# A trunk of convolution and gated recurrence on one core: 32 bytes of padding behind the input tiles and the split weight tiles

## The chip, the cores and the metric

The kernel runs on one core of a Trainium2 chip. The metric is the device time of one execution in microseconds (us). The matrix engine is called PE or TensorE (its weight loads are listed apart, as PEld), the vector engine DVE, the scalar engine ACT, the general engine POOL, and SP issues the DMAs.

## The reference

The reference computes one decoder layer on 1024 tokens of width 1024 in float32. Cut to what matters here:

```python
u = rms_norm(h, ln_g[i])
z = u @ w_in[i]                       # 1024 x 1024 by 1024 x 7168
c_val, c_glu, c_gate, hq, hf, hi, hg = jnp.split(z, split_pts, axis=-1)
y_conv = conformer_conv_branch(c_val, c_glu, c_gate, ...)   # 31 taps, then y @ w_pw2
y_hgrn = hgrn2_branch(hq, hf, hi, hg, ...)                  # 8 heads of 128
h = h + jnp.concatenate([y_conv, y_hgrn], axis=-1) @ w_out[i]
pe = p[i] @ w_pp[i]
gate = jax.nn.sigmoid(rms_norm(h, pe_norm_g[i]) @ w_pg[i])
return rms_norm(h + gate * pe, final_g)
```

Five of these lines hold large matrix products: with `w_in`, `w_pw2`, `w_out`, `w_pp` and `w_pg`.

## The kernel before

**Products in three parts.** A float32 operand of a large product is split into two float32r tiles, a high part `hi` (a rounded copy, made on ACT at L113) and a low part `lo` (the rest, made on DVE at L114). A product is the sum of three matmuls, high by high, high by low and low by high. Every one of these matmuls loads a 128 x 128 block of weights (the stationary operand) and streams 512 columns of float32r past it (the moving operand); for the values of the heads it is 256 columns.

**Where the operands lie.** The input of the layer, normalised and transposed, is held in 32 tiles `uh` and `ul` of 128 partitions by 512 numbers, so of 2048 bytes a partition. They are made in `norm_x` (L173, L174) and come from the pool `up`, which has 32 places under the tag "u". A weight block is made by `prep` (L116 to L123): a `raw` tile, into which SP loads 4096 bytes a partition, and a tile `hi` and a tile `lo` of the same size. Each of these three tags has 3 places in the pool `wp`. Places of one tag lie one behind the other, so they step by 2048 bytes in `up` and by 4096 bytes in `wp`. The slices that the matmuls take out of these tiles begin at multiples of 512 bytes. So do the slices of the tiles of the later stages, which come from `up` and from a third pool, `yp` (L545 to L552, tiles of 2048 bytes).

**Stages.** (1) The layer embedding `p` is multiplied by `w_pp` (L228 to L230) and x is normalised and transposed. (2) In the z stage, head by head, `ztile` takes 128 columns of `w_in` and `product` (L235) multiplies them into two banks of 512 tokens each: 16 rounds of the three matmuls at L241, L242 and L243, with `wh` or `wl` as weights and `uh` or `ul` moving. The values (`values`, L263 to L265) have the roles the other way round: `uh` or `ul` are the weights, and 256 columns of the weight tiles move. Between these products stand the small float32 matmuls of the recurrence (`hgrn`: L295, L383, L409, L426, L427) and transposes (L399, L441, L462, L482). DVE computes the convolution with 29 instructions a head at L452, of which each reads its source `vpad` 4 bytes further on than the one before, and ACT does the activations. (3) `product` again, with `w_pw2` (tiles `pw`). (4) `w_out`, in `accumulate` (L588, L589, L591). (5) `w_pg` (L682 to L684), the gate and the last normalisation.

**What sets the order.** A scheduler orders the instructions of each engine when the program is built. A weight block's load and split are put ahead of time with a raised priority. All large loads are issued by SP's queue. The program reserves 16,384 bytes a partition of the on-chip memory as a scratch area for DMA descriptors; this is the default of the builder called at L715.

Of the kernel before, what the change touches and what calls it, by code (L numbers as in the profile page):

```python
# [16 lines left out]
P = 128  # L17
T = 1024          # tokens
D = 1024          # model width
G = 8             # channel groups, heads, 128-row blocks of T and D  # L20
TAPS = 31
PAD = TAPS - 1
H = 512           # half a row of 1024: one PSUM bank of float32
EPS = 1e-6
# Order of the work of each head and channel group: projections of the GLU gate (u), conv value
# (c), forget gate (f), query (q), values of two heads (v), output gate (g); conv (C); HGRN (H).
ORDER = ("ucfgqvCH", "ucfgqCH") * (G // 2)
# How much later than traced the scheduler takes work that waits on a chain of small steps.
LATER_STATS, LATER_CONV, LATER_HEAD = 50, 330, 240
# columns of the transposed parameter table  # L30
R_CB, R_CG, R_CBETA, R_BPW, R_L0, R_L1, R_ON, R_LN, R_PE = range(TAPS, TAPS + 9)
# [4 lines left out]
def trunk_kernel(ctx: ExitStack, tc: tile.TileContext, x, p, ln_g, w_in, conv_w, conv_b,  # L36
# [25 lines left out]

    # ---------------------------------------------------------------- constants
    ident = cst.tile([P, P], F32, name="ident")
# [5 lines left out]

    # per-channel parameters, channels on partitions
    par = cst.tile([P, G, NR], F32, name="par")
# [3 lines left out]
    def load_params(work):  # L76
        rows = work.tile([NR, D], F32, name="prow")
        nc.sync.dma_start(rows[0:TAPS, :], conv_w[0])
        for r, ap in ((R_CB, conv_b), (R_CG, cnorm_g), (R_CBETA, cnorm_b), (R_BPW, b_pw2),
                      (R_ON, onorm_g), (R_LN, ln_g), (R_PE, pe_norm_g)):  # L80
            nc.sync.dma_start(rows[r:r + 1, :], ap)
        nc.sync.dma_start(rows[R_L0:R_L0 + 2, :], lb_logits)
        pt = bank("t", "pt")
        for g in range(G):
            nc.tensor.transpose(pt[:, g * NR:(g + 1) * NR], rows[:, g * P:(g + 1) * P],
                                ident[:NR, :NR])
        nc.vector.tensor_copy(par, pt[:, :G * NR].rearrange("p (g r) -> p g r", r=NR))
        # lower bound: first row of the softmax over the layers
        l0, l1 = par[:, :, R_L0], par[:, :, R_L1]
        mx = cst.tile([P, G], F32, name="lmx")  # L90
        e0 = cst.tile([P, G], F32, name="le0")
        e1 = cst.tile([P, G], F32, name="le1")
        nc.vector.tensor_tensor(mx, l0, l1, op=ALU.max)
        nc.vector.tensor_tensor(e0, l0, mx, op=ALU.subtract)
        nc.vector.tensor_tensor(e1, l1, mx, op=ALU.subtract)
        nc.scalar.activation(e0, e0, AF.Exp)
        nc.scalar.activation(e1, e1, AF.Exp)
        nc.vector.tensor_tensor(e1, e0, e1, op=ALU.add)
        nc.vector.reciprocal(e1, e1)
        nc.vector.tensor_tensor(lbt, e0, e1, op=ALU.mult)  # L100
        nc.vector.tensor_scalar(oml, lbt, -1.0, 1.0, op0=ALU.mult, op1=ALU.add)
# [14 lines left out]
    def prep(src, shape, name):  # L116
        """A weight block: loaded, and split exactly into two float32r parts."""
        raw = wp.tile(shape, F32, tag="raw", name=name)
        nc.sync.dma_start(raw, src)
        hi = wp.tile(shape, F32R, tag="hi", name=name + "h")  # L120
        lo = wp.tile(shape, F32R, tag="lo", name=name + "l")
        split(hi, lo, raw)
        return hi, lo  # L123
# [6 lines left out]

    # ---------------------------------------------------------------- z phase
    uh = [[None] * G, [None] * G]
    ul = [[None] * G, [None] * G]
    with tc.tile_pool(name="st", bufs=1) as st:
        # layer embedding, projected: kept in DRAM until the gate is known
        KP = p.shape[1] // P
# [29 lines left out]
        def norm_x(hf, xs):  # L166
            """Normalised input of four token blocks, channels on partitions, split."""
            for k in range(G):
                pt = bank("t", f"ut{hf}_{k}")
                for b in range(4):  # L170
                    nc.tensor.transpose(pt[:, b * P:(b + 1) * P], xs[b][:, k * P:(k + 1) * P],
                                        ident)
                uh[hf][k] = up.tile([P, H], F32R, tag="u", name=f"uh{hf}_{k}")  # L173
                ul[hf][k] = up.tile([P, H], F32R, tag="u", name=f"ul{hf}_{k}")  # L174
                nc.scalar.activation(uh[hf][k], pt, AF.Copy, scale=pcol(k, R_LN))
# [5 lines left out]
        load_params(st)  # L181
        # masks[l][s, col]: where the key s is one that the score column couples to, the columns
        # being those of the block of 32 that s lies in
        ones = st.tile([P, 4 * 48], F32, name="ones")
        nc.gpsimd.memset(ones, 1.0)

        def block_mask(dst, first, step_n, step_j, l):
            """Sets dst[s, n, j, i] where s is in the l keys from first + n step_n + j step_j."""
            src = ones[:, :dst.shape[1] * dst.shape[2] * l].rearrange(
# [9 lines left out]
        def own_block(name, mf):  # L199
            """The columns of each row's own block out of those of the four blocks of 32."""  # L200
            n = mf.shape[1] // 4
            own = st.tile([P, n], F32, name=f"own{name}")
            nc.vector.tensor_reduce(own, mf.rearrange("p (b n) -> p n b", b=4), op=ALU.add,
                                    axis=mybir.AxisListType.X)
            msk = cst.tile([P, n], U8, name=f"mask{name}")
            nc.vector.tensor_copy(msk, own)
            return msk
# [27 lines left out]
    def product(wh, wl, mh, ml, tag, name):  # L235
        """Two banks [128 columns of w, 512 tokens] of w^T m."""
        res = []
# [14 lines left out]
    def values(idx, vt):  # L252
        """Two column tiles of z with tokens on partitions."""
        with tc.high_priority(2000):
# [25 lines left out]
    def hgrn(h, QD, K, F, vt, sgT):  # L280
        A, B = AT[h % 2], AB
        # Decayed scores. A level couples the later blocks of l tokens in a parent block to the
        # earlier ones: queries carry the decay since their block of l began (and over the
        # blocks in between), keys the decay until their block of l ends, so that every factor
        # is at most one.
        # Levels within blocks of 32: every block's scores take 48 columns, on its own 32
        # partitions, and go to B[s, chunk, t mod 32].
        blocks = T // 32

        def scores(l, rhs):  # L290
            pt = bank("t", f"sc{h}_{l}")
            pv = pt[:, :G * 48].rearrange("p (c w) -> p c w", c=G)
            for b in range(blocks):
# [4 lines left out]

        # Diagonal and pairs: the keys are the same.
        q01 = QD[:, :, :32].rearrange("p b (n j two) -> p b n j two", j=4, two=2)  # L300
# [9 lines left out]
                                  pv[:, :, 32:])  # L310
        # queries of a level of four blocks: per parent, its blocks 0..3, then 2 and 3 decayed
        # over one more block, then 3 over two more
        Q = wk.tile([P, 7 * T // 4], F32, tag="Q", bufs=2, name=f"Q{h}_2")
# [4 lines left out]
        def pair_keys(l, Fl):  # L318
            """Widens the keys' blocks from l to 2l; the decay over each block of 2l."""
            n = T // (2 * l)  # L320
# [9 lines left out]
        for l in (2, 8):  # L330
# [14 lines left out]
            for d0, j0, cnt in ((1, 0, 3), (2, 3, 2), (3, 5, 1)):  # L345
# [4 lines left out]
                    pv[:, :, :, js])  # L350
            # widen to blocks of 4l
            Q4 = wk.tile([P, 7 * T // 4], F32, tag="Q", bufs=2, name=f"Q{h}_{4 * l}")
# [24 lines left out]
        for l in (32, 64):  # L377
# [14 lines left out]
            Fl = pair_keys(l, Fl)  # L392
        # state after each chunk
        kt = wk.tile([P, G, P], F32, tag="kt", name=f"kt{h}")
# [145 lines left out]

    # ---------------------------------------------------------------- pointwise projection
    yp = ctx.enter_context(tc.tile_pool(name="yp", bufs=32, reuse_waits="tile"))
# [33 lines left out]

    # ---------------------------------------------------------------- output projection
    hs = [hp.tile([P, D], F32, name=f"h{tb}") for tb in range(G)]
# [3 lines left out]
    def accumulate(zs, hf, k, wh, wl, first, last):  # L582
        """zs: {(token block, column half): bank}."""
        for b in range(4):
# [34 lines left out]
    def norm_T(hf):  # L619
        """Scaled residual of 4 token blocks, channels on partitions, split; its RMS in rs."""  # L620
        hh = [None] * G
# [34 lines left out]

    # ---------------------------------------------------------------- gated layer embedding
    gh = [[None] * G, [None] * G]
# [8 lines left out]
    for tb in range(G):  # L667
# [5 lines left out]
        ot = wp.tile([P, D], F32, tag="lo", name=f"ot{tb}")  # L673
        # the last block ends in narrower pieces, so that less work follows the last product
        pieces = (H, H) if tb < G - 1 else (H, H // 2, H // 2)
# [54 lines left out]
```

## Time and profile before

| | us |
|---|---|
| median of the 2 runs | 1147.24 |
| the 2 runs | 1146.36 and 1148.12 |
| span of the profiled execution | 1146.5 |

The page of the profiled execution gives its span from the first to the last instruction; the two timed runs lie within 1.6 us above it and 0.2 us below it, so no time of note lies around the span. In a row of a profile, "L241" is line 241 of the kernel, "xN" a count, "out<-in" the tiles written and read (of a matmul: output, then moving operand and weights). A matmul's listed duration includes the time in which its last columns run through the array, and the next one starts before it ends: what a stream of matmuls costs is read from start to start.

### The profile page before, as it was taken

What the parts mean: (1) busy time and instruction counts of PE and PEld (TensorE: products, weight loads), DVE (VectorE), ACT (ScalarE), POOL (GpSimd) and SP (SyncE); (2) the same over time, 40 slices, a digit from 0 to 9 for tenths busy, and PEclk for the clock granted to TensorE, in tenths of its full rate; (3) what the DMA queues carried; (4) which work ended last, traced back from release to release, by engine and by line L of the source; (5) the groups of instructions that cost most, each with busy time, mean ns of one, the idle gap of its engine ahead of it and who ended that gap; (6) DMA issues with size and microseconds to landing.
All of it is one profiled execution on the core that took longest, in us unless ns stands there. A gap on an engine that the chain in (4) does not pass through costs nothing.

```text
span 1146.5 us, 17744 instructions
## 1 busy us (share of the span) xinstructions
PE 1124.8 (98%) x7408; PEld 945.6 (82%) x7408; DVE 739.5 (65%) x1145; ACT 443.0 (39%) x811; POOL 72.0 (6%) x107
## 2 busy tenths in 40 slices
PE   6999999999999999999999999999999999999997
PEld 4888978889888789788898788888888888887886
DVE  3659579998499996599993896242334325226444
ACT  4823244253354442344532632442123324126333
POOL 3100001001001010010010010000000001001000
PEclk9899999999999999999999999999999999999999
DMA  7611121211111112111111112277335632334221
GB/s 247 236 37 55 37 66 30 74 55 39 55 57 56 59 35 74 56 37 56 57 56 56 57 56 93 74 242 254 110 92 165 195 99 77 107 109 149 92 92 56
DMA packets 85715, 104.60 MB, mean 91 GB/s; under 512 B 3290, under 2 KB 65754, under 8 KB 85634
## 3 DMA queue, kind: packets, MB, share of 16 engines
q1 hardware_dynamic: 85634, 103.46, 28.1%
q8 instruction: 58, 0.95, 0.3%
q14 instruction: 23, 0.19, 0.1%
HBM read 82.48 MB, written 20.97 MB: 90 GB/s over the span
## 4 chain that ended last, share of the span: by engine, by line
PE 89%; DVE 6%; DMA 2%; ACT 1%; issue 1%; SPq 0%; POOL 0%; POOLq 0%; ACTq 0%
PE z L241 14%; PE z L242 14%; PE z L243 14%; DVE y L452 4%; PE v L264 3%; PE v L265 3%; PE v L263 3%; PE pg L683 3%; PE pg L684 3%; PE pg L682 3%; PE oA L591 3%; PE pw L243 3%; PE pw L241 3%; PE oA L589 3%; PE oA L588 3%; PE pw L242 3%
## 5 line engine op out<-in xcount | busy, mean ns | idle before, releaser
L452 DVE SCALAR_TENSOR_TENSOR y<-vpad,par,y 128x1024 f32<-128x1024 f32 x232 | 288.8, 1278 | 1.1
L682 PE MATMUL pg<-gh,hh 128*128 128x512 f32 (+1 forms) x136 | 51.4, 378 | 0.0
L683 PE MATMUL pg<-gl,hh 128*128 128x512 f32 (+1 forms) x136 | 51.4, 378 | 0.0
L684 PE MATMUL pg<-gh,hl 128*128 128x512 f32 (+1 forms) x136 | 51.3, 377 | 0.0
L519 DVE TENSOR_TENSOR vpad<-z,gl 128x512 f32<-128x512 f32 x16 | 11.0, 691 | 42.7 <-PE z L243 42.7
L263 PE MATMUL v<-wv_0h,uh 128*128 128x256 f32 x128 | 36.7, 287 | 0.0
L265 PE MATMUL v<-wv_0h,ul 128*128 128x256 f32 x128 | 36.5, 285 | 0.0
L264 PE MATMUL v<-wv_0l,uh 128*128 128x256 f32 x128 | 36.5, 285 | 0.0
L263 PE MATMUL v<-wv_1h,uh 128*128 128x256 f32 x128 | 36.2, 283 | 0.0
L264 PE MATMUL v<-wv_1l,uh 128*128 128x256 f32 x128 | 36.2, 283 | 0.0
L265 PE MATMUL v<-wv_1h,ul 128*128 128x256 f32 x128 | 36.2, 283 | 0.0
L266 ACT ACTIVATE vt<-v 128x256 f32<-128x256 f32 x32 | 12.2, 382 | 58.9 <-PE v L265 58.9
L688 DVE TENSOR_TENSOR gt<-gt,pet 128x512 f32<-128x512 f32 (+1 forms) x17 | 11.2, 661 | 36.1 <-ACT gt L687 36.1
L108 POOL TENSOR_SCALAR ro<-sso 128x8 f32<-128x8 f32 x8 | 8.4, 1054 | 389.9 <-ACT on L129 389.9
L475 DVE TENSOR_SCALAR y<-yt,mv,ry 128x128 f32<-128x128 f32 x64 | 23.5, 404 | 13.1 <-POOL ry L109 13.1
L570 DVE SCALAR_TENSOR_TENSOR sgr<-pw,par,sgr 128x512 f32<-128x512 f32 x16 | 12.0, 750 | 30.1 <-PE pw L243 30.1
L437 ACT ACTIVATE on<-o,ro 128x128 f32<-128x128 f32 x64 | 18.5, 386 | 29.0 <-POOL ro L109 29.0
L682 PEld LDWEIGHTS pg<-gh,hh 128*128 128x128 f32 x136 | 25.6, 188 | 4.7
L683 PEld LDWEIGHTS pg<-gl,hh 128*128 128x128 f32 x136 | 25.6, 188 | 4.7
L684 PEld LDWEIGHTS pg<-gh,hl 128*128 128x128 f32 x136 | 25.6, 188 | 4.5
L483 ACT ACTIVATE yc<-yn,par 128x512 f32<-128x512 f32 x16 | 12.5, 778 | 39.8 <-PE yn L482 39.8
L129 ACT ACTIVATE on<-o 128x128 f32<-128x128 f32 x64 | 16.9, 278 | 23.3 <-PE up L409 18.9
(802 smaller groups left out, 3463.6 us busy)
## 6 DMA issues: line engine op xcount, KB each, us to landing
wz<-in_w_in_dram SPq DMA_DIRECT2D x48, 512.0 KB
wo<-in_w_out_dram SPq DMA_DIRECT2D x32, 512.0 KB
xt<-in_x_dram SPq DMA_DIRECT2D x8, 512.0 KB
pe_d<-pes SPq DMA_DIRECT2D x8, 512.0 KB
wv<-in_w_in_dram SPq DMA_DIRECT2D x8, 512.0 KB
yc_d<-yc SPq DMA_DIRECT2D x8, 512.0 KB
yh_d<-sgT SPq DMA_DIRECT2D x8, 512.0 KB
sg_d<-sgc SPq DMA_DIRECT2D x8, 512.0 KB
```

The lines of the kernel that those rows point to most:

```text
L241: mm(z, lhsT=wh[:, k, :], rhs=mh[hf][k], start=k == 0, stop=False)
L242: mm(z, lhsT=wh[:, k, :], rhs=ml[hf][k], start=False, stop=False)
L243: mm(z, lhsT=wl[:, k, :], rhs=mh[hf][k], start=False, stop=k == G - 1)
L263: mm(z, lhsT=uh[hf][k][:, c], rhs=wh, start=k == 0, stop=False)
L264: mm(z, lhsT=uh[hf][k][:, c], rhs=wl, start=False, stop=False)
L265: mm(z, lhsT=ul[hf][k][:, c], rhs=wh, start=False, stop=k == G - 1)
L452: nc.vector.scalar_tensor_tensor(y[j % 2], vp[:, j:j + T], pcol(g, j), y[j % 2], op0=ALU.mult, op1=ALU.add)
L588: mm(z, lhsT=mixh[hf][k][:, c], rhs=wh[j], start=first, stop=False)
L589: mm(z, lhsT=mixh[hf][k][:, c], rhs=wl[j], start=False, stop=False)
L682: mm(z, lhsT=hh[k][:, c], rhs=gh[j][k][:, o:o + w], start=k == 0, stop=False)
L683: mm(z, lhsT=hh[k][:, c], rhs=gl_[j][k][:, o:o + w], start=False, stop=False)
L684: mm(z, lhsT=hl[k][:, c], rhs=gh[j][k][:, o:o + w], start=False, stop=k == G - 1)
```

## The change

The tiles `uh` and `ul` get 8 float32 more than they use, so their 32 places step by 2080 bytes. The tiles `hi` and `lo` of `prep` are made as flat tiles of 1032 numbers and cut back to 1024, so their 3 places step by 4128 bytes. Views of the same shape as before are taken of them, and every instruction works on the same elements. The `raw` tiles and the tiles of `yp` keep their size. The descriptor scratch goes from 16,384 to 2,048 bytes a partition, which makes room: the program took all but some 600 of the bytes of a partition before, and the padding needs 38 times 32 = 1216. Every tile behind the scratch area moves down accordingly. Later tiles that use the places of "u", "hi" and "lo" (`mc`, `hh`, `hl`, `gt`, `ot`) start where those places start. In the built program before, the moving operand and the weights of each of the 4,728 float32r matmuls begin at addresses that differ by a multiple of 512 bytes; after the change that holds for 206 of them, 2,232 differ by an even multiple of 32 bytes (206 among them) and 2,496 by an odd one. The operands of the float32 matmuls and transposes (L399, L409) lie in other pools and differ by no multiple of 512 before. The instructions of each engine and their order stay as they were (6272 matmuls of the program in the same order, as all others), and so do the semaphores that they wait for.

```diff
+STEP = 8
...
     def prep(src, shape, name):
         raw = wp.tile(shape, F32, tag="raw", name=name)
         nc.sync.dma_start(raw, src)
-        hi = wp.tile(shape, F32R, tag="hi", name=name + "h")
-        lo = wp.tile(shape, F32R, tag="lo", name=name + "l")
+        n = shape[1] if len(shape) == 2 else shape[1] * shape[2]
+        hi = wp.tile([P, n + STEP], F32R, tag="hi", name=name + "h")[:, :n]
+        lo = wp.tile([P, n + STEP], F32R, tag="lo", name=name + "l")[:, :n]
+        if len(shape) == 3:
+            hi, lo = (t.rearrange("p (k c) -> p k c", k=shape[1]) for t in (hi, lo))
         split(hi, lo, raw)
         return hi, lo
...
-                uh[hf][k] = up.tile([P, H], F32R, tag="u", name=f"uh{hf}_{k}")
-                ul[hf][k] = up.tile([P, H], F32R, tag="u", name=f"ul{hf}_{k}")
+                uh[hf][k] = up.tile([P, H + STEP], F32R, tag="u", name=f"uh{hf}_{k}")[:, :H]
+                ul[hf][k] = up.tile([P, H + STEP], F32R, tag="u", name=f"ul{hf}_{k}")[:, :H]
...
-    nc = _bacc.Bacc("TRN2", target_bir_lowering=False, num_devices=1)
+    nc = _bacc.Bacc("TRN2", target_bir_lowering=False, num_devices=1,
+                    dynamic_dma_scratch_size=2048)
```

## Rows read from the trace of the kernel before

**Rows 1.** The page: span, and busy time, share and instructions of each engine.

```profile
span 1146.5 us, 17744 instructions
...
PE 1124.8 (98%) x7408; PEld 945.6 (82%) x7408; DVE 739.5 (65%) x1145; ACT 443.0 (39%) x811; POOL 72.0 (6%) x107
```

**Rows 2.** The page: shares of the chain that ended last, by engine.

```profile
PE 89%; DVE 6%; DMA 2%; ACT 1%; issue 1%; SPq 0%; POOL 0%; POOLq 0%; ACTq 0%
```

**Rows 3.** Busy time by stretch: length, engines (instructions), granted clock, DMA share, GB/s.

```profile
0.00:30.00 30.00, 19.26 (x77) 15.06 (x78) 11.83 (x23) 13.44 (x21) 11.38 (x30) 0.96 0.79 251
...
315.00:415.00 100.00, 99.62 (x933) 81.71 (x933) 96.22 (x149) 47.25 (x85) 5.70 (x4) 1.00 0.17 54
...
760.00:860.00 100.00, 100.00 (x443) 82.84 (x442) 36.20 (x46) 26.68 (x38) 0.00 (x0) 1.00 0.52 171
```

**Rows 4.** Timeline in the z stage: start us, us, engine, line, operation, tiles.

```profile
142.04 0.39 PE L243 MATMUL z<-uh,wz1l 128*128 128x512 f32 x1
142.04 0.19 PEld L241 LDWEIGHTS z<-uh,wz1h 128*128 128x128 f32 x1
142.27 0.39 PE L241 MATMUL z<-uh,wz1h 128*128 128x512 f32 x1
...
149.97 0.39 PE L242 MATMUL z<-ul,wz1h 128*128 128x512 f32 x1
```

**Rows 5.** Timeline of the values' matmuls, 256 columns wide.

```profile
105.77 0.28 PE L263 MATMUL v<-wv_0h,uh 128*128 128x256 f32 x1
105.77 0.19 PEld L264 LDWEIGHTS v<-wv_0l,uh 128*128 128x128 f32 x1
...
106.73 0.28 PE L265 MATMUL v<-wv_0h,ul 128*128 128x256 f32 x1
```

**Rows 6.** Eight transposes in the timeline, and the line's own view (min/median/max ns).

```profile
175.33 1.03 PE L399 MATMUL ktp<-ident,K 128*128 128x128 f32 x8
...
L399 PE MATMUL ktp<-ident,K x64: 270/272/273, 175.3 to 723.5; 128*128 128x128 f32 x64
```

**Rows 7.** Whole span, one line each of L228, L241, L263, L588, L682 (count behind PE).

```profile
0.00:1146.50 1146.50, 14.07 (x32) 6.63 (x32) 1.00 0.29 91
0.00:1146.50 1146.50, 356.76 (x896) 168.41 (x896) 1.00 0.29 91
0.00:1146.50 1146.50, 72.93 (x256) 49.11 (x256) 1.00 0.29 91
0.00:1146.50 1146.50, 99.88 (x256) 48.08 (x256) 1.00 0.29 91
0.00:1146.50 1146.50, 51.41 (x136) 25.60 (x136) 1.00 0.29 91
```

**Rows 8.** Weight loads by line and shape: busy us, mean ns, idle before.

```profile
L241 PEld LDWEIGHTS z<-uh,wz26h 128*128 128x128 f32 x16 | 3.0, 189 | 0.6
...
L409 PEld LDWEIGHTS up<-vt,kt 128*128 128x128 f32 x112 | 20.6, 189 | 4.2 <-ACT kt L401 0.3
```

**Rows 9.** DVE: the convolution's line (min/median/max ns) and one split, by line.

```profile
L452 DVE SCALAR_TENSOR_TENSOR y<-vpad,par,y x232: 1264/1278/1290, 75.1 to 685.1; 128x1024 f32<-128x1024 f32 x116
...
L114 DVE TENSOR_TENSOR wz48l<-wz,wz48h 128x1024 fp32r<-128x1024 f32 x1 | 1.2, 1226 | 7.3 <-ACT wz48h L113 7.3
```

**Rows 10.** DMA queues: packets, MB, share of 16 engines.

```profile
q1 hardware_dynamic: 85634, 103.46, 28.1%
```

## The prediction

> **What bounds the kernel now.** I read the page's busy times first, then the chain that ended last, then busy time by stretch, and then single matmuls in the timeline. The reader is to see that PE is busy for 1124.8 of 1146.5 us [rows 1] and holds 89% of the chain; DMA has 2% of it [rows 2]. By stretch it is the same: PE is busy for 99.62 of 100 us in the middle of the z stage and for all of 100 us in the `w_out` stage [rows 3]. DVE comes near only in places (96.22 of the 100 us from 315), and the DMA engines only in the opening, at a share of 0.79 [rows 3]. So the change can win or lose only by what it does to the distance between matmuls, or by making another engine so much slower that it overtakes PE.
>
> That distance is the number of the case. In the z stage the matmuls at 142.04 and 149.97 us are the ends of 35 steps (L241 to L243 in turn) [rows 4]: 7.93 / 35 = 226.6 ns a step. At the granted clock of 1.00, that is 2.4 GHz, 512 columns stream in 213.3 ns, so 13.3 ns of each step is something else. The values stream 256 columns (106.7 ns), and 8 steps take 106.73 - 105.77 = 0.96 us [rows 5], 120 ns each: again 13.3 ns over. Eight transposes of 128 columns, which are float32 and pass twice (106.7 ns), end after 1.03 us of which the last one's own duration is 0.272 [rows 6]: (1030 - 272) / 7 = 108.3 ns a step, only 1.6 ns over. So float32r matmuls pay about 11.7 ns more than these do.
>
> **The change part by part.** It removes and adds no instruction, no transfer and no wait, and it moves none. What it can change is how long an instruction takes at its new addresses, and how DMAs are issued with a smaller scratch. The sum is made against the profiled execution, 1146.5 us, which is 0.7 us below the median of the runs, 1147.24; I put its difference on the median.
>
> *Matmuls.* There are 3 x (32 + 896 + 256 + 256 + 136) = 4,728 of float32r, since each row stands for one of a stage's three lines [rows 7]. Before, the two operands of every one of them lie a multiple of 512 bytes apart, and the weights of the next matmul begin to load at the same 0.01 us at which the current one starts to stream (142.04 and 142.04, 105.77 and 105.77) [rows 4, 5]. If the two streams, starting in step, collide in the memory, the 11.7 ns could be that collision, and the change would end it. If it belongs to float32r itself, the change does nothing. The trace of before can't settle this, because no float32r matmul in it has operands out of step, and the transposes differ in both respects. So I bound it from both sides by the nearest rows: gain at most 4,728 x 11.7 = 55.3 us; loss at most as much again as today's overhead for those matmuls whose operands lie an odd multiple of 32 apart, 2,496 x 13.3 = 33.2 us.
>
> I take zero, for three reasons. The overhead is the same 13.3 ns for a stream of 2048 bytes as for one of 1024 bytes, so it goes with the instruction and not with how long the two streams run beside each other. The 35 steps also run through weight slices that lie 512, 1024 and 1536 bytes apart within 2048, and still come to one mean that equals the values'. And a weight load takes 189 ns in the z stage, in step, and 189 ns at L409, where the operands lie out of step [rows 8]; if two reads held each other up I would expect the load to show some of it.
>
> On this place the Trainium skill has two rules that pull apart. "TensorE: Matmul & The Clock Gate", section "Back-to-back issue gap", gives a step of N / 2.4 + 2.5 ns at full clock, which is 215.8 ns for 512 columns; by it 226.6 is too long and the sum would be an estimated 4,728 x 10.8 = 51 us of avoidable time, which bears out the collision. The same page, section "Step-by-step: what each phase is for", says that loading the next weights takes no read bandwidth from the running matmul because PE has two read ports; by it there is no collision and the sum is zero. The trace agrees with the first for the transposes (1.6 ns over) and contradicts it for float32r, which the page's figure was not measured on.
>
> *DVE and ACT.* The 166 splits on DVE now read or write a tile that may begin 32 bytes off a multiple of 64. DVE shows no sign of caring: at L452 the source moves by 4 bytes from one instruction to the next, through 29 different places, and all 232 durations lie between 1264 and 1290 ns [rows 9]. A spread of 2% on a split of 1226 ns would be 25 ns, times 166 is 4 us of DVE in 1146, where DVE is busy 65% [rows 1]; PE's work covers it. I put it at zero; where the cover is thin, from 315 to 415 us, DVE has 3.8 us left [rows 3], and a seventh of 4 us fits. For ACT, which only writes the padded tiles, I see no row that would say otherwise, and it is busy 39%.
>
> *The scratch.* All 85,634 packets of the kernel's transfers go through one queue that the page calls hardware_dynamic [rows 10]. Whether it keeps anything in the scratch area the trace doesn't show. If not, the cost is zero, which I take, because DMA is 2% of the chain and its share is under a fifth for most of the z stage [rows 2, 3].
>
> The sum is 0 + 0 + 0: 1147 us, and its own range, from the runs' spread and the few us of the covered terms, is 1143 to 1152.
>
> **The rivals.**
>
> *A: the collision is real, and any shift of phase ends it.* Then all but 206 of 4,728 matmuls lose 11.7 ns: 52.9 us, so 1094. For it speaks that 13.3 ns goes with in-step operands wherever it is seen and 1.6 ns with out-of-step ones, and that PE has nothing else in its way. Against it, the three reasons above. In the z stage DVE would take some of it back: from 315 us on PE would need about 95 of 100 us where DVE needs 96.2 [rows 3], which costs 1 or 2 us. I say 1095.
>
> *B: the collision is real, but depends on the position within 64 bytes only.* Then the 2,496 matmuls at an odd multiple of 32 are freed: 2,496 x 11.7 = 29.2 us, so 1118. The same rows speak for it, and the finer the pattern in memory, the less the equal overhead of all slices says against it.
>
> *C: starts off a multiple of 64 bytes cost a restart.* Here the 2,496 matmuls with one operand 32 bytes off pay the overhead twice: 33.2 us, so 1180, slower. The place is every stage, the price is 13.3 ns, and it decides from 22.9 / 2,496 = 9 ns a matmul, where the time passes 2%. Against it: nothing of the kind shows on DVE at any of 29 places [rows 9]; PE's float32r stream may still have less slack than DVE's.
>
> *D: the smaller scratch throttles the DMAs*, so that the change does something else than it says. The opening is the place: its first 30 us run at a DMA share of 0.79, and PE is busy for only 19.26 of them [rows 3]. At half the rate 24 us of transfers become 48, so up to 24 us more there; the `w_out` stage at 0.52 [rows 3] would just be covered. That is 1171, and it needs a queue held to half its rate.
>
> **How the numbers follow.** A difference of under 2%, 23 us, is about what a measurement of this kernel can tell from no change. My forecast, no change, has 0.69; A 0.11 and B 0.13; C 0.04 and D 0.03. A and B both end over 2% faster (1095 and 1118 against 1124.3), so faster is 0.24. C and D at their full price end over 2% slower (1180 and 1171 against 1170.2): 0.07. The same is 0.69. The range goes down to 1116, which takes in B, and leaves A out; upward to 1158, about a third of C's price, which leaves out 0.05 or so. What is left out is 0.16 to 0.18. The predicted time is that of the likeliest case, 1147.
>
> **What would show it right or wrong.** If I am right, the timeline of the z stage still has a step of 226 to 227 ns for every pair of tiles, whichever places they have, the weight loads still take 188 or 189 ns, and the splits 1226. If A or B is right, steps near 215 ns appear: under A for nearly all, under B for every other place, so that lines with `uh` and with `ul` moving differ. If C is right, steps near 240 ns appear for the same half. If D is right, matmuls are untouched and the DMA share of the opening falls while PE's idle time there grows. Any change in the step of float32r matmuls by more than 5 ns over most tiles makes the prediction wrong.

## The result, and the profile after

The changed kernel takes 1159.12 us (median of 2 runs, 1159.01 to 1159.23) against 1147.24 us before: 11.9 us more, a ratio of 1.0106 with a 95% interval of 1.0089 to 1.0122. That is less than 2%, but its interval leaves 1 out, and the time lies 1 us above the range that was forecast. No difference was forecast.

Of the page after, the span, the busy times, the chain by engine and the DMA queue stand here beside [rows 1], [rows 2] and [rows 10]; the lines of the program are 4 further on than before.

```profile
span 1157.5 us, 17744 instructions
...
PE 1140.0 (98%) x7408; PEld 945.3 (82%) x7408; DVE 738.7 (64%) x1145; ACT 443.1 (38%) x811; POOL 72.6 (6%) x107
...
q1 hardware_dynamic: 85634, 103.46, 27.8%
...
PE 89%; DVE 6%; DMA 2%; ACT 1%; issue 0%; SPq 0%; POOLq 0%; POOL 0%; ACTq 0%
```

Instructions, packets and megabytes are the same. The span is 11.0 us longer and PE is busy for 15.2 us more, while weight loads, DVE, ACT and POOL moved by less than 1 us, and the shares of PE, DVE and DMA in the chain did not move. So the time went into PE's matmuls and nowhere else. The same three stretches as in [rows 3]:

```profile
0.00:30.00 30.00, 21.10 (x78) 16.34 (x79) 12.10 (x23) 13.74 (x24) 11.40 (x30) 0.96 0.77 251
...
315.00:415.00 100.00, 99.77 (x929) 81.15 (x928) 95.83 (x149) 46.64 (x85) 5.70 (x4) 1.00 0.17 54
...
760.00:860.00 100.00, 100.00 (x433) 80.88 (x432) 37.01 (x49) 27.55 (x41) 0.00 (x0) 1.00 0.54 177
```

The reader is to look at the counts and not at the busy shares: in the `w_out` stage PE is busy for all of 100 us in both kernels, but gets through 433 matmuls where it got through 443. That is 230.9 ns each for 225.7. The granted clock is 1.00 in both, so the engine isn't slower, its matmuls stand further apart. The opening moves as many GB/s as before (251) at the same DMA share within 0.02.

In the z stage, the timeline has these two matmuls, with 25 others between them and no gap; they answer to [rows 4]:

```profile
144.86 0.39 PE L245 MATMUL z<-uh,wz1h 128*128 128x512 f32 x1
...
150.88 0.39 PE L247 MATMUL z<-uh,wz1l 128*128 128x512 f32 x1
```

26 steps in 6.02 us are 231.5 ns a step, where before they were 226.6. Over the whole span, the first lines of the four products (L245, L267, L592, L686) answer to [rows 7]:

```profile
0.00:1157.50 1157.50, 360.45 (x896) 168.52 (x896) 1.00 0.28 90
...
0.00:1157.50 1157.50, 72.33 (x256) 48.24 (x256) 1.00 0.28 90
...
0.00:1157.50 1157.50, 101.17 (x256) 48.09 (x256) 1.00 0.28 90
...
0.00:1157.50 1157.50, 51.82 (x136) 25.55 (x136) 1.00 0.28 90
```

Three of them grew and the values shrank. Summed over the three lines of each triple, z and `w_pw2` together took 9.1 us more, `w_out` 3.6, `w_pg` 1.5, and the values 1.7 less: 12.5 us, which covers the 11.9 that were measured. (The lines of `w_pp` are busy for 2.0 us more, in the opening; from start to start they take 0.4 us less.) The weight loads, the convolution and the split of [rows 8] and [rows 9]:

```profile
L245 PEld LDWEIGHTS z<-uh,wz26h 128*128 128x128 f32 x16 | 3.0, 189 | 0.6
...
L456 DVE SCALAR_TENSOR_TENSOR y<-vpad,par,y 128x1024 f32<-128x1024 f32 x232 | 288.8, 1278 | 1.1
...
L115 DVE TENSOR_TENSOR wz48l<-wz,wz48h 128x1024 fp32r<-128x1024 f32 x1 | 1.2, 1226 | 7.5 <-ACT wz48h L114 7.5
```

All as before: 189 ns, 1278 ns, 1226 ns. The listed duration of a matmul does move: 395 ns here, 389 ns for the same 16 matmuls before. First after, then before:

```profile
L245 PE MATMUL z<-uh,wz3h 128*128 128x512 f32 x16 | 6.3, 395 | 0.0
...
L245 PE MATMUL pw<-ych,wpw3h 128*128 128x512 f32 x16 | 6.3, 393 | 0.0
```

```profile
L241 PE MATMUL z<-uh,wz3h 128*128 128x512 f32 x16 | 6.2, 389 | 0.0
```

Where nothing interrupts the stream, the step is this duration less about 162 ns (389 - 226.6 before), so the column of mean durations shows the step of every tile at a glance. It is used below.

### The profile page after: what moved, and what is told of

It is laid out like the page before. It is cut to its first block, busy times and chain, and to the rows that moved or that the text cites. A ratio compares the mean times of both kernels' runs of the same rounds, so it can differ in the third digit from the quotient of the medians.

```text
span 1157.5 us, 17744 instructions
## 1 busy us (share of the span) xinstructions
PE 1140.0 (98%) x7408; PEld 945.3 (82%) x7408; DVE 738.7 (64%) x1145; ACT 443.1 (38%) x811; POOL 72.6 (6%) x107
## 4 chain that ended last, share of the span: by engine, by line
PE 89%; DVE 6%; DMA 2%; ACT 1%; issue 0%; SPq 0%; POOLq 0%; POOL 0%; ACTq 0%
PE z L245 14%; PE z L246 14%; PE z L247 14%; DVE y L456 4%; PE v L267 3%; PE v L268 3%; PE v L269 3%; PE pw L245 3%; PE pg L688 3%; PE pw L246 3%; PE pg L687 3%; PE oA L592 3%; PE oA L595 3%; PE pg L686 3%; PE oA L593 3%; PE pw L247 3%
## 5 line engine op out<-in xcount | busy, mean ns | idle before, releaser
L456 DVE SCALAR_TENSOR_TENSOR y<-vpad,par,y 128x1024 f32<-128x1024 f32 x232 | 288.8, 1278 | 1.1
L686 PE MATMUL pg<-gh,hh 128*128 128x512 f32 (+1 forms) x136 | 51.8, 381 | 0.0
L267 PE MATMUL v<-wv_0h,uh 128*128 128x256 f32 x128 | 36.4, 284 | 0.0
L267 PE MATMUL v<-wv_1h,uh 128*128 128x256 f32 x128 | 35.9, 281 | 0.0
L270 ACT ACTIVATE vt<-v 128x256 f32<-128x256 f32 x32 | 12.2, 383 | 57.7 <-PE v L269 57.7
L686 PEld LDWEIGHTS pg<-gh,hh 128*128 128x128 f32 x136 | 25.6, 188 | 5.2
L487 ACT ACTIVATE yc<-yn,par 128x512 f32<-128x512 f32 x16 | 12.5, 779 | 40.5 <-PE yn L486 40.5
```

Source lines behind the costliest of these rows:

```text
L267: mm(z, lhsT=uh[hf][k][:, c], rhs=wh, start=k == 0, stop=False)
L456: nc.vector.scalar_tensor_tensor(y[j % 2], vp[:, j:j + T], pcol(g, j), y[j % 2], op0=ALU.mult, op1=ALU.add)
L686: mm(z, lhsT=hh[k][:, c], rhs=gh[j][k][:, o:o + w], start=k == 0, stop=False)
```

## The experiments

**1. Matmuls alone, with the distance of the operands as the only variable (map1).** Groups of 20 float32r matmuls into one bank, with the same two operands each time, the weights taken `s` and the moving operand `m` numbers into two tiles that begin a multiple of 256 bytes apart. Groups differ in `s` (wshift, 32 bytes a group; fine, 4 bytes), in `m` (mshift), in both (both), in the columns (narrow: 256), or take two slices in turn (turns, turnm). A matmul is called in step here when its weights and its moving operand begin a multiple of 256 bytes apart.

```python
for r in range(rep):
    m, s = mv[r % len(mv)], st[r % len(st)]
    mm(z[:, :n], lhsT=W[:, s:s + P], rhs=X[:, m:m + n], start=r == 0, stop=r == rep - 1)
...
    z = group(f"wshift{chr(97 + i // 16)}{chr(97 + i % 16)}", [0], [8 * i])
...
    z = group(f"mshift{chr(97 + i)}", [8 * i], [0])
...
    z = group(f"both{chr(97 + i)}", [8 * i], [8 * i])
...
    z = group(f"narrow{chr(97 + i)}", [0], [8 * i], n=256)
```

> A kernel of float32r matmuls alone (the trunk is left out, its output is one bank's numbers): groups of 20 matmuls of 512 columns, each with its own weight load; from group to group the weight slice, the moving slice or both begin 32 bytes (in one series 4 bytes) further on. Theory 1, the two reads of PE meet in the memory, so the step depends on how far apart they begin: 'both' groups all alike at the 226.6 ns of the kernel before, 'wshift' and 'mshift' groups between 224 and 238 ns, the same values at the same distance. Theory 2, starts that are not multiples of 64 bytes cost by themselves: every second group slower by some 5 to 10 ns, in 'both' as in the others. Theory 3, neither, the padding isn't the cause: 226.6 ns in all groups of 512 columns.

In the timeline, a group is one row: its start, and its busy time from the first start to the last end, which is 19 steps and one duration. The weights begin 0, 32, 256 and 288 bytes behind the moving operand:

```profile
26.94 4.70 PE L57 MATMUL wshiftaa<-X,W 128*128 128x512 f32 x20
...
31.48 4.82 PE L57 MATMUL wshiftab<-X,W 128*128 128x512 f32 x20
...
64.07 4.70 PE L57 MATMUL wshiftai<-X,W 128*128 128x512 f32 x20
...
68.61 4.82 PE L57 MATMUL wshiftaj<-X,W 128*128 128x512 f32 x20
```

(4.70 - 0.389) / 19 = 226.9 ns and (4.82 - 0.395) / 19 = 232.9 ns: 32 bytes cost 6 ns, and 256 bytes bring the old step back. From the starts of the single matmuls, the mean steps by the distance of the weights behind the moving operand, modulo 256 bytes, are (an entry moves by up to 0.7 ns with the choice of which steps of a group are averaged):

| bytes | 0 | 32 | 64 | 96 | 128 | 160 | 192 | 224 |
|---|---|---|---|---|---|---|---|---|
| 512 columns, ns | 226.7 | 233.3 | 233.3 | 234.7 | 232.2 | 233.6 | 228.7 | 233.3 |
| 256 columns, ns | 120.0 | 118.4 | 117.8 | 117.2 | 118.9 | 119.9 | 113.3 | 116.6 |

The pattern repeats every 256 bytes up to 1024. Moving the other operand gives the mirror image within about 1 ns (228.8 where it stands 64 bytes on). Moving both alike leaves 226 to 227 ns, after some seven steps of 223 to 236 ns at a group's start; so it is not the starts by themselves that count (theory 2), and theory 3 is out as well. In steps of 4 bytes, up to 60, only the distance 0 gives 226.7, all others 230 to 235. With two slices in turn, those 256 bytes apart settle at 226.7. The rows by line and shape show the width's part: at 0 and at 192 bytes the narrow groups have

```profile
L57 PE MATMUL narrowa<-X,W 128*128 128x256 f32 x20 | 2.6, 283 | 0.0
...
L57 PE MATMUL narrowg<-X,W 128*128 128x256 f32 x20 | 2.4, 276 | 0.0
...
L57 PEld LDWEIGHTS wshiftab<-X,W 128*128 128x128 f32 x20 | 3.8, 188 | 0.9
...
L57 PEld LDWEIGHTS wshiftaa<-X,W 128*128 128x128 f32 x20 | 3.8, 188 | 0.8
```

So in step is the best place for 512 columns and, together with 160 bytes, the worst for 256. And the weight load takes 188 ns whether the step is 226.7 or 233.3: its duration can't tell.

**2. The scratch alone (scratch_only).** No padding, the smaller scratch stays. Of `hi` and `lo`, and of `uh` and `ul`, the edit is the same, and one line of each stands here.

```diff
-        hi = wp.tile([P, n + STEP], F32R, tag="hi", name=name + "h")[:, :n]
+        hi = wp.tile([P, n], F32R, tag="hi", name=name + "h")[:, :n]
...
-                uh[hf][k] = up.tile([P, H + STEP], F32R, tag="u", name=f"uh{hf}_{k}")[:, :H]
+                uh[hf][k] = up.tile([P, H], F32R, tag="u", name=f"uh{hf}_{k}")[:, :H]
```

> The smaller descriptor scratch without any padding; all places step by 2048 and 4096 bytes again. Theories 1 and 2: as the kernel before, within 0.2% of 1147 us, with steps of 226 to 227 ns. If the scratch is the cause: 1159 us with the steps of the kernel before and more idle time of PE.

1147.14 us against 1147.36, ratio 0.9999 (0.9989 to 1.0008). The scratch, and with it the place of every tile behind it, has no part in the loss.

**3. and 4. One padding at a time (u_only, w_only).** The first takes `n + STEP` in `prep` back to `n` and pads `uh` and `ul` alone; the second is the reverse. Again `lo` and `ul` are edited like `hi` and `uh`.

```diff
-        hi = wp.tile([P, n + STEP], F32R, tag="hi", name=name + "h")[:, :n]
+        hi = wp.tile([P, n], F32R, tag="hi", name=name + "h")[:, :n]
```

```diff
-                uh[hf][k] = up.tile([P, H + STEP], F32R, tag="u", name=f"uh{hf}_{k}")[:, :H]
+                uh[hf][k] = up.tile([P, H], F32R, tag="u", name=f"uh{hf}_{k}")[:, :H]
```

> Padding behind the input tiles alone. Theory 1: the distance of the two reads changes for every product of the z stage and w_pw2 keeps its own, so most of the loss stays, 1154 to 1159 us. Theory 2: only the tiles at an odd multiple of 32 (ul) pay, so lines with ul moving are slower by some 10 ns and the others not; about 1154 us.

> Padding behind the split weight tiles alone. Theory 1: most products have weights or moving operands from these tiles, so some of the loss comes here too, 1150 to 1160 us, and with few distances each pair of tiles has one step of its own that doesn't wander from round to round. Theory 2: only the second of three places (32 bytes off) pays, a third of the weight blocks, 1151 us.

u_only takes 1155.81 us, ratio 1.0077 (1.0061 to 1.0093); w_only 1160.08, ratio 1.0118 (1.01 to 1.0136), 0.1 us above the range expected of it. Either padding does most of the harm or all of it by itself, and the two don't add: 8.5 and 12.7 us alone, 11.9 together. That is what a distance does, which either operand can spoil. Two stages in which one padding touches no operand decide it. In u_only, the matmuls of `w_pw2` (moving `ych` from the unpadded pool `yp`, weights unpadded) are back at their 389 ns, and `w_pg`, whose weights `hh` and `hl` use the places of "u" (its moving `gh` and `gl` lie in `yp`), is not (51.82 us against 51.41 in [rows 7]). In `w_out` half the weights (`mc`) use the places of "u" and half (`mh`) lie in `yp`: in one and the same product, the first kind is slower and the second isn't:

```profile
L245 PE MATMUL pw<-ych,wpw3h 128*128 128x512 f32 x16 | 6.2, 389 | 0.0
...
L592 PE MATMUL oB<-wo_3h,mch 128*128 128x512 f32 x16 | 6.3, 394 | 0.0
...
L592 PE MATMUL oB<-wo_4h,mhh 128*128 128x512 f32 x16 | 6.2, 389 | 0.0
...
0.00:1155.30 1155.30, 51.82 (x136) 25.55 (x136) 1.00 0.28 91
```

Theory 2 expected only the lines with `ul` moving to be slower; in the uninterrupted streams of z the means of the three kinds of matmul rise by 3.0 to 4.6 ns each. In w_only it is the other way round: `w_pg` (L686) is back at 51.40 us, and z is not:

```profile
L245 PE MATMUL z<-uh,wz3h 128*128 128x512 f32 x16 | 6.3, 394 | 0.0
...
0.00:1157.20 1157.20, 51.40 (x136) 25.60 (x136) 0.99 0.28 90
```

**5. Other widths, and bfloat16 (map2).** Map1's group at 128 to 512 columns, and with bfloat16 copies, again matmuls alone.

```diff
+    for n, c in ((128, "one"), (192, "onehalf"), (256, "two"), (320, "twohalf"), (384, "three"),
+                 (448, "threehalf"), (512, "four")):
+        for i in range(8):
+            z = group(f"{c}{chr(97 + i)}", 0, 8 * i, n=n)
+    for n, c in ((256, "btwo"), (512, "bfour")):
+        for i in range(8):
+            z = group(f"{c}{chr(97 + i)}", 0, 16 * i, n=n, x=X16, w=W16)
```

> A kernel of matmuls alone again (the trunk is left out, its output is one bank's numbers): float32r with 128 to 512 columns in steps of 64, each at eight distances of the weights from the moving operand, 0 to 224 bytes; then bfloat16 with 256 and 512 columns at the same distances. Reading a, each weight load of 512 bytes holds the moving stream up by a fixed amount per instruction that depends on the distance alone: the time over the columns' own is 13.3 ns at distance 0 for every width, and 20 +/- 2 ns at the others. Reading b, it depends on where the moving stream ends too, since its last bytes overlap the next load: the order of the distances changes from width to width, as 192 bytes is best for 256 columns (6.7 ns over) and 0 for 512. For bfloat16, which moves half the bytes per column, reading a and b both expect less over, under 8 ns, and a spread over the distances of under 3 ns.

Four groups in the rows by line and shape, 512 columns at distances 0 and 96 and the same in bfloat16:

```profile
L63 PE MATMUL fourd<-X,W 128*128 128x512 f32 x20 | 4.8, 396 | 0.0
L63 PE MATMUL foura<-X,W 128*128 128x512 f32 x20 | 4.7, 391 | 0.0
L63 PE MATMUL bfoura<-Xb,Wb 128*128 128x512 bf16 x20 | 4.5, 379 | 0.0
L63 PE MATMUL bfourd<-Xb,Wb 128*128 128x512 bf16 x20 | 4.5, 379 | 0.0
```

With bfloat16 the step is 215.8 or 215.9 ns at every distance (109.1 for 256 columns), 2.4 to 2.5 over its columns. With float32r the time over the columns is 13.3 at all eight distances for 320 columns, 13.3 to 16.7 for 384, 13.3 to 20.0 for 448, and 6.7 to 13.3 for 256. At 128 and 192 columns the step is 111.7 ns whatever the distance, so something else bounds it there; whether it is the loading of the weights, no run tried. So the overhead neither goes with the instruction nor grows with the columns: it depends on width and distance together, and on the type.

**6. Padding of a whole period (step256).** The change with 256 bytes for 32.

```diff
-STEP = 8
+STEP = 64
```

> The change with 256 bytes of padding in place of 32, on the same tiles; the distance of the two reads is a multiple of 256 bytes for all 4,728 float32r matmuls, but of 512 no longer for all. The memory repeats every 256 bytes (theory 1 with the period that the map showed): 1147 us, steps of 226 to 227 ns throughout, ratio 1.000. If padding or staggered places cost as such, or the period is 512 or longer: 1152 to 1160 us.

1147.06 us against 1147.4, ratio 0.9998 (0.9989 to 1.0007). The places are staggered as in the change, by 256 bytes each in place of 32, and the loss is gone; L245 as a whole is back at 356.99 us (356.76 in [rows 7]).

```profile
L245 PE MATMUL z<-uh,wz3h 128*128 128x512 f32 x16 | 6.2, 389 | 0.0
...
0.00:1144.00 1144.00, 356.99 (x896) 168.44 (x896) 0.99 0.28 91
```

**7. and 8. The values out of step on purpose (values64, values64b).** Since 256 columns gain out of step, the tiles that move in the values begin 64 bytes into their places, everything else stays in step. values64b leaves "u" as it was and pads the weights alone.

```diff
-    def prep(src, shape, name):
+    def prep(src, shape, name, off=0):
...
-        hi = wp.tile([P, n + STEP], F32R, tag="hi", name=name + "h")[:, :n]
+        hi = wp.tile([P, n + STEP], F32R, tag="hi", name=name + "h")[:, off:off + n]
...
+                       ... [P, 4, 2 * P], f"wv{idx}_{j}", off=16)
```

> As step256, and the split weight tiles of the values alone start 64 bytes into their places, so that for 768 matmuls of 256 columns the weights lie 192 bytes (modulo 256) past the moving operand. By the map (113.3 ns at that distance, 120.0 at 0) 768 x 6.7 = 5.1 us less: 1142 us, ratio 0.9955, with steps of 113 to 114 ns at the three lines of the values and 226 to 227 elsewhere. If the map of one repeated pair doesn't carry over to operands that change from matmul to matmul: anything from 1143 to 1147 us.

> As values64, with the places of the tiles at steps of 2048 and 4608 bytes, so that the 768 matmuls of the values have one and the same distance within 512 bytes (448) and not two in turn (192 and 448). If it was the mixture that kept values64 at 118 ns a step: 113.3 ns here, 5 us less than before, 1142 us, ratio 0.9955. If it is that the operands change from matmul to matmul (weights and moving operand each in turn from the hi and the lo tile): 118 ns as in values64, 1145.7 us, ratio 0.9987.

1146.51 us, ratio 0.9995 (0.9986 to 1.0004), and 1145.6 us, ratio 0.9984 (0.9975 to 0.9993). The second is faster than the kernel before, by 2.0 us against the runs of it that stand beside it (1147.61); of the first the interval takes in 1. In both, the values take 118 ns a step, not the 113.3 of map1, and 1.6 us less than before from start to start; what else lies between the two times is not the values. 768 matmuls by 2 ns are 1.5 us, where 6.7 ns would have been 5.1. The line of L267 in values64b:

```profile
0.00:1144.30 1144.30, 72.01 (x256) 47.93 (x256) 0.99 0.28 91
```

**9. The trunk's own sequences (map3).** Matmuls alone, but with the kernel's loops: the triples of the values and of z, with the two weight tiles 32 bytes times 0 to 7 out of step, each by itself.

```python
for i in range(8):
    for j in range(8):
        z = values(f"v{chr(97 + i)}{chr(97 + j)}", 8 * i, 8 * j, 2)
...
        z = ztile(f"z{chr(97 + i)}{chr(97 + j)}", 8 * i, 8 * j)
```

> Matmuls alone, in the two patterns of the trunk (the rest is left out, the output is one bank's numbers): first the values' triples (weights uh, uh, ul; moving wh, wl, wh of 256 columns), 64 groups of 48 with wh and wl each at 0 to 224 bytes past the phase of the input tiles; then the z stage's triples with 512 columns, 64 groups of 24. Theory 1: each pair of offsets has its own mean step, 113 to 122 ns for the values and 226 to 235 for the z stage, with both at 0 giving 120 and 226.7; no z group is better than 226 ns. If the trunk's 118 ns at distance 192 comes from the pattern, the values' group with both at 64 (distance 192) shows 118 too; else 113.3.

The values give means of 117.0 to 120.8 ns over the 64 combinations, 120 in step and 117.8 with both tiles at 64 bytes. So the 118 belongs to the loops of the values and not to the work around them. z gives 228.7 over a whole group in step, 226.9 over its last 15 steps, which is the best of its 64 combinations either way; the others give 228.9 to 235.2 over a whole group. The views of the tiles in step (zaa) and with both weight tiles 32 bytes on (zbb), as min/median/max of the durations and first to last start:

```profile
L75 PE MATMUL zaa<-U,Wh x8: 387/389/397, 402.2 to 407.0; 128*128 128x512 f32 x8
```

```profile
L75 PE MATMUL zbb<-U,Wh x8: 392/395/396, 452.2 to 457.1; 128*128 128x512 f32 x8
```

**10. One distance for all (offset32).** Padding of 256 bytes, but every `hi` and `lo` begins 32 bytes into its place: where they meet `uh`, `ul` or `ych`, all distances are the same.

```diff
-STEP = 8
+STEP = 64
...
-        hi = wp.tile([P, n + STEP], F32R, tag="hi", name=name + "h")[:, :n]
-        lo = wp.tile([P, n + STEP], F32R, tag="lo", name=name + "l")[:, :n]
+        hi = wp.tile([P, n + STEP], F32R, tag="hi", name=name + "h")[:, 8:8 + n]
+        lo = wp.tile([P, n + STEP], F32R, tag="lo", name=name + "l")[:, 8:8 + n]
```

> step256 (all places a multiple of 256 bytes apart), with every split weight tile starting 32 bytes into its place: one constant distance in place of sixteen. Theory 1, by the maps: 2,688 matmuls with the weights 32 bytes past the moving operand at 233.4 for 226.7 ns (+18.0 us), 768 of w_out with the moving operand 32 bytes past (+6.6 ns, +5.1 us), 768 of the values at 117.7 for 120 (-1.8 us), w_pg unchanged: 1168 us, at least 1162, so slower than the change itself. If what costs is that the places differ from tile to tile (many distances), a constant offset costs nothing: 1147 us.

1161.46 us, ratio 1.0122 (1.0106 to 1.0137), just under the lower bound that was expected. The step where nothing interrupts is 233.2 or 233.3 ns in z, `w_pw2` and `w_out`, as map1 has for 32 bytes, and 116.7 in the values; `w_pg`, whose operands lie in the places of "u" and in `yp` and so still a multiple of 256 bytes apart, is as before. The sum of the maps was 21.3 us and the run shows 14.2; most of what is missing is in z, 9.2 us from start to start where the map's price makes 15.2 (the section on why says where it went).

```profile
L245 PE MATMUL z<-uh,wz3h 128*128 128x512 f32 x16 | 6.3, 396 | 0.0
L245 PE MATMUL pw<-ych,wpw3h 128*128 128x512 f32 x16 | 6.3, 396 | 0.0
...
L686 PE MATMUL pg<-gh,hh 128*128 128x512 f32 x120 | 46.9, 391 | 0.0
```

A constant distance costs more than the change's many. So it isn't the variety of places that costs, nor a change of distance from one matmul to the next.

**11. Everything 32 bytes on (shift_all32).** No padding; a tile of 32 bytes ahead of all others.

```diff
+    cst.tile([P, 8], F32, name="shift")
```

> No padding, but a tile of 32 bytes ahead of everything, so that every operand of every matmul starts at an odd multiple of 32 bytes and all distances stay multiples of 256. Theory 1: 1147 us, ratio 1.000, steps of 226 to 227 ns. Theory 2, starts off a multiple of 64 bytes cost by themselves (rival C of the prediction): up to 4,728 x 13.3 ns more, 1160 to 1210 us.

1147.3 us against 1147.27, ratio 0.9999 (0.9989 to 1.0009). Every operand now begins off a multiple of 64 bytes, and nothing happens: only where the two stand to each other counts.

## Why the prediction was wrong, point by point

**The step that failed is the matmul term, taken as zero.** The overhead of a float32r matmul does not go with the instruction alone: it depends on how far apart its two operands begin, and the change moved most of them out of the place that is best for 512 columns. The steps of the changed kernel in uninterrupted streams are 224 to 240 ns (mean 231.8, against 227.4 for the same matmuls before) for 512 columns, and 112 to 126 (mean 118, against 120) for 256. By stage, matmul by matmul against before, from start to start, this is +6.6 us in z, +2.2 in `w_pw2`, +3.2 in `w_out`, +1.7 in `w_pg`, -1.4 in the values: 12.2 in place of the term's zero. The products of `w_pp` and the float32 matmuls take 1.2 us less, which leaves the 11.0 between the two spans.

With the means of map1 put in for the distance that each matmul has in the built program (its addresses stand in no profile), the same five would be 9.6, 2.4, 4.3, 2.0 and -1.7, or 16.6. The sign of every stage holds; the size doesn't in z and `w_out`. For z the starts in the trace show where the 3 us went. Its products are interrupted by the matmuls of the recurrence. The 1,331 matmuls that stand ten places or more behind an interruption go from 226.7 to 231.6 ns and make all of the 6.6 us. The 619 nearer to one took 230.7 ns already before, in step, much as the first seven steps of map1's groups do, and go to 231.9 (+0.8 us). The 354 right beside an interruption take 0.8 us less. Why a stream in step needs some matmuls to settle is open.

**The three reasons for zero.** The first, that the overhead goes with the instruction since it is 13.3 ns at both widths, fell with map2: 13.3 is what both widths happen to have in step, 448 columns have 16 there, and bfloat16 pays 2.5 with the same instruction. The second, that slices 512, 1024 and 1536 bytes apart share one step, was a true reading of the wrong sample: with a period of 256 bytes all of them are the same place. The prediction did say that no float32r matmul before was out of step, and then let the three reasons stand for a measurement. The third, the 189 ns of the weight loads, says nothing at 512 columns: loads stay at 187 to 189 ns while the steps go from 226.7 to 235. Only the values' loads show something, 192 ns before (49.11 / 256 in [rows 7]) and 188 after (48.24 / 256), and they were not looked at.

**The price of 11.7 ns.** The gain bound of 55.3 us and the rivals A and B take it from the transposes, as a step of 108.3 ns less 106.7 for a float32 stream that passes twice. No run shows that second pass for them: the trace lists each float32 product of the recurrence twice (7,408 matmuls listed for the program's 6,272), but each transpose at L399 once [rows 6]. And map2 has 128 columns of float32r, for which 53.3 ns is the columns' own time, at 111.7 ns a step at every distance. So at this width something other than the stream can set the step, and the 1.6 ns is not known to be the transposes' overhead. What the runs do show of another type is bfloat16, 2.5 ns against 13.3 at 512 columns.

**The bounds.** The loss of 11.9 us lies within the bounds of -55.3 and +33.2 us; the price per matmul out of step was set at 13.3 ns for half of them, and was 2 to 8 ns in map1 for every distance but 0, so for odd and even multiples alike, less a gain of 2 in the values. That the loss fell inside is no merit of that term: its price was too high and its count too low. The range's upper end took a third of rival C's price, which was 1 us too little.

**The rivals.** A and B read the 13.3 ns of in-step matmuls as a collision that any shift would end. The place was right, the sign wrong: for 512 columns in step is the best place, and only the values, at 256 columns, behave as A said, at 2 ns instead of 11.7. C had the right sign, for starts off a multiple of 64 bytes; shift_all32 puts every start there at no cost, and in map1's table even multiples of 32 (64 and 128 bytes, 233.3 and 232.2 ns) cost about as much as odd ones. D fell with scratch_only.

**The two rules weighed.** The bfloat16 groups take 215.8 ns for 512 columns. "TensorE: Matmul & The Clock Gate" of the Trainium skill, section "Back-to-back issue gap", gives N / 2.4 + 2.5 ns for isolated matmuls at full clock, which is the same 215.8 ns. For float32r no run here reached it, the least overhead at 512 columns being 13.3 ns. The same page's "Step-by-step: what each phase is for" lets the weight load take no read bandwidth from the running matmul. The bfloat16 groups agree (no distance matters), the float32r groups don't: 226.7 against 233.3 ns, with nothing changed but where the weights begin.

**What was right.** DVE and ACT cost nothing (1278 and 1226 ns on DVE as before, ACT busy for 443.1 us against 443.0), the DMAs neither, the order and the waits gave no new stall: the loss sits in the step of the matmuls alone, where the prediction said that it would have to. Its own test, steps moved by over 5 ns over most tiles, comes out on the edge. Against the stretch of [rows 4] the mean of the streams with 512 columns is 5.2 ns longer (231.8 for 226.6); matmul by matmul against before it is 4.4, and 42% moved up by more than 5.

**Open.** What in the hardware repeats every 256 bytes; why a float32r matmul still pays 13.3 ns in step; why the values get 118 ns at a distance where one pair of operands, repeated, gets 113.3. No run here looks inside.

## What to carry to other kernels

A trace in which all operands stand in one phase can't say what the phase is worth; if a change moves addresses, measure matmuls alone at several distances first. For float32r with 512 columns, keep moving operand and weights a multiple of 256 bytes apart (pad by 256 bytes or not at all), and with 256 columns try 64 bytes on the moving side (it was worth 2 ns a matmul here). Read the step from start to start, not the busy share or the weight load, which show nothing.

## What the runs showed of the hardware that was not expected

The step of a float32r matmul depends on the distance of its two operands with a period of 256 bytes, by up to 8 ns in 227, while moving all of them on alike by 32 bytes changes nothing (0.9999). After an interruption a stream in step takes some ten matmuls to come down to 226.7 ns (230.7 on the mean of those ten in z). The best distance turns with the width: 0 for 512 columns (226.7 ns), 192 for 256 columns (113.3 for 120.0), none for 320. At 128 and 192 columns a step takes 111.7 ns at every distance. bfloat16 is indifferent at 215.8 and 109.1 ns.
